# S5 stage of a two-layer diffusion backbone: phase tables summed earlier and loaded, period reordered, inputs ahead of transposes, own residual buffers, modulation products in the GLU stage

## The chip, the cores and the metric

The kernel runs on one core of one Trainium2 chip. The metric is the device time of one execution in microseconds (us). The core has five engines with in-order queues: PE (TensorE, matmuls; PEld is its weight load), DVE (VectorE), ACT (ScalarE), POOL (GpSimd) and SP (SyncE), which here issues every DMA. "L1806" is line 1806 of the kernel before.

## The reference

Two layers over 1024 latent tokens with 256 context tokens in front, 1024 channels, in fp32. Layer 0 mixes tokens with differential attention, layer 1 with a bidirectional S5 state-space scan and a GLU; each mixer is followed by a squared-ReLU MLP (1024 to 4096 to 1024). Cut to what the change touches:

```python
for i in range(2):
    mod_l = silu(c) @ ada_w[i] + ada_b[i]           # six vectors of 1024: sh1 s1 g1 sh2 s2 g2
    h = rmsnorm(x, g0) * (1 + s1) + sh1
    y = attention(h) if i == 0 else s5_mixer(h)
    x = x + g1 * rmsnorm(y, g1n)
    h = rmsnorm(x, g2n) * (1 + s2) + sh2
    x = x + g2 * rmsnorm(square(relu(h @ w1)) @ w2, g3n)

# s5_mixer, for both directions d, 64 groups of 16 channels, 64 complex states per group
h_t = lam_bar * h_{t-1} + B u_t                     # recurrence over time
y   = Re(C h_t) summed over d, + D * u
g   = gelu(y);  o1, o2 = split(g @ w_glu);  return o1 * sigmoid(o2)
```

The kernel cuts time into chunks of 8 tokens (so 160 chunks, context first) and turns the complex recurrence over chunks into a real one: the chunk inputs are rotated by minus a phase (theta times the chunk index), scanned with a real decay, and rotated back. That is why the kernel needs, for each group of four state rows, a table of phases and its sine and cosine.

## The kernel before, in words

The stages run one after the other: attention; the first MLP's up part (`mlp0_up`, matmuls against w1 with hi/lo split operands: L132 to L134 are the three products of such a split, L137 and L138 make the two halves of an operand on ACT and DVE); its down part (`mlp0_down`); the S5 scan (`s5`); the GLU (`glu`); the second MLP up and down. Around the matmuls, `self.bg` holds generators of background work, of which a step is emitted after each piece of main work. The order on the engines is chosen by a scheduler, except inside `with self.manual()`, where the written order is kept; only SP's order is still chosen there.

**Phases.** In `mlp0_down` the background step `s5_phases` (L1199) lets POOL fill two int32 tables by doubling additions (L1209, L1212, L1214): A (128 x 10) and B (128 x 16) for each partition. They go to device memory (`ptd`, 13 KB per partition, 1.7 MB) and come back before `s5`. A phase table of one period n and direction d, 128 x 640, is then made inside `s5` by one POOL addition of broadcast slices, A + B (`phase`, L1777). There are three buffers for phases and their cosines (`phs`).

**The period.** `s5` runs n = 0 to 15 (four groups each), plus a tail for the GELU. For each n and d:
- `trig` (ACT, L1781 to L1784): sine of the half phase, sine, square, and 1 - 2 times it, which is the cosine. `decay` (ACT, L1811) fills the scan's decay.
- `inputs(n, d)` (PE, L1797): 8 matmuls, each two passes in the trace, into two PSUM banks.
- `rotate(n, d)` (DVE, L1806): PSUM inputs times cosine and times sine, into t1 and t2. Then POOL adds them (L1887 for d = 0, L1896 for d = 1).
- `scan` (DVE, L1815), from t1 into t2 with the decay.
- `back` (L1823): t2 times cosine on DVE, t2 times sine on POOL.

`outputs(n)` (PE, L1829 and L1832) multiplies the rotated-back states of both directions with C and adds the direct term. The GELU of period n - 2 follows (ACT L1870, L1883, L1889; DVE L1882, L1904), then four PE transposes (`tr`, L1836) and a split of the result (ACT L1840, DVE `lo` L1841), which is the GLU's operand.

The two directions have separate t1 buffers per parity of n, but d = 0 has one t2 for both parities (FD 12.5), and so has d = 1 (FD 20).

**Modulation of layer 1.** Its segments 2 to 5 (g1, sh2, s2, g2) are eight halves of 1024 x 512 each. Each is loaded in four pieces of 512 KB into one of two sets of buffers and multiplied by 32 small fp32 matmuls (L247, 64 passes in the trace), copied (L251), transposed (L254) and added into `modc` (L256). They stand in the periods n = 8 to 17, after `outputs` and ahead of `tr`.

**From `mlp0_down` to `s5`.** Ten row tiles (two of context, eight latent) are normalised by steps of `m0_tile`: `residual` (L1710) writes y = w * r + x; `second` (ACT L1715 and DVE or POOL L1716) squares y and writes w = y * A; `modulate` (L1719) writes y = w * r + B **into the same y** whose value the residual step stores to `xb` by DMA. So `modulate` waits until that store has landed. Four 32 x 32-block transposes (L1678) put the result into U, which `inputs` reads. The last two tiles, 6 and 7, use W 12 and H 52 for x.

**GLU.** `glu` runs two groups of four row tiles; in each, four column blocks nb with 24 matmuls per tile (L132 to L134) and their operands' splits. The row g1 is spread to all partitions at its start (`rows_out`, `row_bc`).

Of the kernel before, what the change touches and what calls it, by code (L numbers as in the profile page):

```python
# [6 lines left out]
F32 = mybir.dt.float32  # L7
F32R = mybir.dt.float32r
I32 = mybir.dt.int32
# [61 lines left out]
class Prog:  # L71
# [171 lines left out]
    def ada_half_products(self, ws, l, seg, half, acc, t=None):  # L243
# [5 lines left out]
        if t is None:  # L249
            t = self.adat[:, 0:128]  # L250
            nc.scalar.activation(t, acc, AF.Copy)  # L251
        else:
            nc.vector.tensor_copy(t, acc)
# [696 lines left out]
    def s5_prep(self):  # L950
# [67 lines left out]
        self.dma(self.phd, pc)  # L1018
# [180 lines left out]
    def s5_phases(self, o):  # L1199
# [3 lines left out]
        B, P, P16 = (self.fv(x, *d).bitcast(I32) for x, d in ((o, (128, 16)), (o + 8, (128,)), (o + 8.5, (128,))))  # L1203
        self.dma(self.fv(o + 9, 128), self.phd)
        nc.vector.tensor_copy(P, self.fv(o + 9, 128))
# [11 lines left out]
        fill(B, 16, P)  # L1217
        g(P16, B[:, :, 8], B[:, :, 8], ALU.add)
        self.dma(self.ptd[:, 5 * KB : 13 * KB], B.rearrange("p a b -> p (a b)"))
        yield  # L1220
        A = self.fv(o, 128, 10).bitcast(I32)
        fill(A, 10, P16)
        self.dma(self.ptd[:, 0 : 5 * KB], A.rearrange("p a b -> p (a b)"))
        yield
# [8 lines left out]
    def phase_c(self):  # L1233
        nc, I = self.nc, self.I
# [259 lines left out]
    def mlp0_up(self):  # L1494
# [8 lines left out]
                                   [self.rows_out(1, acc)], [self.w2_sums(fu(17.5, 2, 1024))])]  # L1503
        for p in range(self.HEAD // 2, 16):
# [76 lines left out]
    def mlp0_down(self):  # L1581
# [6 lines left out]
        self.bg = [self.s5_phases(40), self.s5_tables(0, self.bank(3), self.bank(2))]  # L1588
# [67 lines left out]
    def m0_buffers(self, i):  # L1656

        f, w = lambda x: self.fv(x, 1024), lambda: self.wv(12, 1024)
        h = lambda: self.hv(52, 1024).bitcast(F32)
        return {0: lambda: (f(40), f(44)), 1: lambda: (f(48), f(52)), 2: lambda: (h(), w()), 3: lambda: (f(40), f(44)),  # L1660
                8: lambda: (f(52), w()), 9: lambda: (h(), f(52)), 4: lambda: (w(), f(0)), 5: lambda: (h(), f(4)),
                6: lambda: (w(), f(8)), 7: lambda: (h(), f(12))}[i]()
# [17 lines left out]
    def m0_tile(self, i, b=None):  # L1680
# [28 lines left out]
        def residual():  # L1709
            v.scalar_tensor_tensor(y, w, r, x, ALU.mult, ALU.add)  # L1710
            if i < 8:
                self.tile_dma(self.xb, i, y, store=True)

        def second():
            act.activation(junk, y, AF.Square, scale=1.0 / 32, accum_out=ms)  # L1715
            (pool if i in (9, 5) else v).tensor_tensor(w, y, A, ALU.mult)  # L1716

        def modulate():
            v.scalar_tensor_tensor(y, w, r, B, ALU.mult, ALU.add)  # L1719
# [15 lines left out]
    def s5(self):  # L1735
# [10 lines left out]
        At, Bt = self.fv(42.5, 128, 10).bitcast(I32), self.fv(47.5, 128, 16).bitcast(I32)  # L1746
# [559 lines left out]
```

## Time and profile before

| | us |
|---|---|
| measured, 3 runs | 2934.82, 2941.13, 2941.93 (median 2941.13) |
| profiled execution, first to last instruction (span) | 2929.2 |
| the median less that span (work around the span) | 11.9 |
| `mlp0_up` | about 1080 to 1455 |
| `mlp0_down`, to its last product | about 1455 to 1870.5 |
| first rotation of `s5` | 1893.91 |
| last rotation pair of n = 15, d = 0 | 2074.93 |
| last transposes of `s5` end | 2101.3 |
| first GLU matmul | 2102.94 |

The page gives the span alone for the profiled execution; its own device time is taken as the span with the same 11.9 us around it, that is 2941.1 us, equal to the median. A row of the windows view gives, for a stretch of the span, the busy time of each engine (with its count of instructions), the granted TensorE clock, the share of time in which the 16 DMA engines were busy, and GB/s. A row of the timeline gives start, length, engine, line, operation, output <- input, shape, and in brackets how long the engine was idle before it and what it waited for. A row of groups gives all instructions of one line and shape with their busy time and mean length in ns. Over the whole span PE is busy 2739.6 us (94%), DVE 2021.3 (69%), ACT 1367.5 (47%) and POOL 1062.1 (36%).

### The profile page before, as it was taken

Reading aid. Unit: us, or ns where it says so; the run is one execution under the profiler, and the core shown is the slowest. Engines: PE = TensorE matmul, PEld = TensorE weight load, DVE = VectorE, ACT = ScalarE, POOL = GpSimd, SP = SyncE. Lnnn points to the kernel's source line nnn. Section 1 sums busy time; section 2 is a strip of 40 time slices with the busy share of each in tenths; the row PEclk is TensorE's granted clock in tenths of the full one; section 3 lists DMA queues with packets and bytes.
Section 4 is the critical chain, followed back from the end, with each engine's and each line's share of the span. In section 5 each row is a group of like instructions: output and inputs, shape, how many; then the busy total and the mean of one; then the engine's idle time right before and its main releaser. Section 6 shows DMA issues by size and latency. Waiting matters only on the chain.

```text
span 2929.2 us, 43646 instructions
## 1 busy us (share of the span) xinstructions
PE 2739.6 (94%) x15200; PEld 2287.5 (78%) x15200; DVE 2021.3 (69%) x2956; ACT 1367.5 (47%) x2555; POOL 1062.1 (36%) x923
## 2 busy tenths in 40 slices
PE   5998999999988999999999999688899899999999
PEld 3687888788777887878877778588788678878887
DVE  5355777777764477676688768699743687758566
ACT  3424555555553663333444435377543643345443
POOL 2213666666553700000020004499410543326324
PEclk8999999999989999999999999899999999999999
DMA  9956455555744448886699988468834254467544
GB/s 250 292 181 205 139 164 169 162 149 162 220 145 152 140 152 303 303 291 243 228 299 293 274 241 258 153 200 264 282 124 136 72 175 159 148 213 256 159 139 141
DMA packets 454122, 588.44 MB, mean 201 GB/s; under 512 B 62742, under 2 KB 299532, under 8 KB 450700
## 3 DMA queue, kind: packets, MB, share of 16 engines
q1 hardware_dynamic: 453900, 585.63, 63.6%
q8 instruction: 120, 1.97, 0.3%
q14 instruction: 102, 0.84, 0.1%
HBM read 398.48 MB, written 182.82 MB: 198 GB/s over the span
## 4 chain that ended last, share of the span: by engine, by line
PE 66%; DMA 12%; DVE 10%; issue 4%; ACT 4%; SPq 2%; POOL 2%; DVEq 0%; ACTq 0%; POOLq 0%
PE PS L132 19%; PE PS L133 18%; PE PS L134 18%; SPq L80 2%; PE PS L520 2%; PE PS L1797 2%; ACT F L543 2%; PE PS L1832 1%; PE PS L566 1%; DVE F L533 1%; DVE R L138 1%; DVE H L138 1%; PE PS L202 1%; DMA U<-in_mlp_w 1%; DMA U<-Aa 1%
## 5 line engine op out<-in xcount | busy, mean ns | idle before, releaser
L132 PE MATMUL PS<-H 128*128 128x512 f32 x1048 | 412.0, 395 | 7.7 <-DVE FD L1604 5.0
L133 PE MATMUL PS<-H 128*128 128x512 f32 x1048 | 410.4, 392 | 0.0
L134 PE MATMUL PS<-H 128*128 128x512 f32 x1048 | 409.8, 392 | 0.0
L132 PE MATMUL PS<-H,R 128*128 128x512 f32 (+1 forms) x836 | 311.2, 378 | 18.5 <-ACT F L579 13.7
L133 PE MATMUL PS<-H,R 128*128 128x512 f32 (+1 forms) x836 | 303.8, 363 | 1.1 <-POOL H L138 1.1
L134 PE MATMUL PS<-H,R 128*128 128x512 f32 (+1 forms) x836 | 303.6, 364 | 0.0
L137 ACT ACTIVATE R<-W 128x512 fp32r<-128x512 f32 (+1 forms) x203 | 142.9, 711 | 208.7 <-PE PS L133 114.9
L132 PEld LDWEIGHTS PS<-H 128*128 128x128 f32 x1048 | 197.9, 189 | 52.4 <-DVE FD L1604 5.3
L134 PEld LDWEIGHTS PS<-H 128*128 128x128 f32 x1048 | 197.7, 189 | 42.5 <-issue 1.0
L133 PEld LDWEIGHTS PS<-H 128*128 128x128 f32 x1048 | 197.9, 189 | 41.2 <-issue 1.2
L132 PE MATMUL PS<-R,H 128*128 128x512 f32 x532 | 214.7, 407 | 7.4 <-ACT H L137 6.0
L543 ACT ACTIVATE F<-F,stat 128x1280 f32<-128x1280 f32 x128 | 174.3, 1362 | 83.8 <-DVE F L533 83.5
L133 PE MATMUL PS<-R,H 128*128 128x512 f32 x532 | 210.8, 397 | 0.0
L134 PE MATMUL PS<-R,H 128*128 128x512 f32 x532 | 208.3, 395 | 0.0
L137 ACT ACTIVATE H<-U 128x640 fp32r<-128x640 f32 x216 | 132.8, 677 | 144.2 <-PE PS L133 110.7
L132 PEld LDWEIGHTS PS<-H,R 128*128 128x128 f32 x836 | 160.7, 193 | 47.6 <-ACT F L579 15.1
L138 DVE TENSOR_TENSOR H<-W,H 128x512 fp32r<-128x512 f32 (+1 forms) x137 | 128.6, 949 | 93.6 <-ACT H L137 93.6
L138 DVE TENSOR_TENSOR R<-W,R 128x512 fp32r<-128x512 f32 (+1 forms) x166 | 150.8, 915 | 60.8 <-ACT R L137 53.5
L533 DVE TENSOR_SCALAR_CACHE_REDUCE F<-PS 128x1280 f32<-128x1280 f32 x128 | 185.1, 1482 | 9.1 <-PE PS L520 8.9
L138 DVE TENSOR_TENSOR H<-U,H 128x640 fp32r<-128x640 f32 x216 | 163.4, 793 | 39.5 <-ACT H L137 39.3
L580 POOL TENSOR_SCALAR R<-F 128x256 fp32r<-128x256 f32 (+1 forms) x128 | 122.8, 959 | 172.1 <-ACT F L579 149.1
L134 PEld LDWEIGHTS PS<-H,R 128*128 128x128 f32 x836 | 160.7, 192 | 25.9 <-issue 0.8
(477 smaller groups left out, 6818.0 us busy)
## 6 DMA issues: line engine op xcount, KB each, us to landing
W<-in_mlp_w SPq DMA_DIRECT2D x184, 256.0 KB, 3.1
U<-Aa SPq DMA_DIRECT2D x108, 320.0 KB, 5.0
Aa<-FU SPq DMA_DIRECT2D x91, 320.0 KB, 4.6
Ad<-F SPq DMA_DIRECT2D x112, 256.0 KB, 3.2
W<-Ad SPq DMA_DIRECT2D x112, 256.0 KB, 2.8
W<-in_ada_w SPq DMA_DIRECT2D x32, 512.0 KB, 6.9
FU<-in_mlp_w SPq DMA_DIRECT2D x32, 512.0 KB, 6.3
Ta<-FU SPq DMA_DIRECT2D x16, 1024.0 KB, 5.6
```

The costliest lines, as they stand in the source:

```text
L80: return self.nc.sync.dma_start(out=out, in_=in_)
L132: mm(out, ah, bh, start=first, stop=False, **kw)
L133: mm(out, ah, bl, start=False, stop=False, **kw)
L134: mm(out, al, bh, start=False, stop=last, **kw)
L137: self.nc.scalar.activation(hi, src, AF.Copy)
L138: (lo_eng or self.nc.vector).tensor_tensor(lo, src, hi.bitcast(F32), ALU.subtract)
L202: self.nc.tensor.matmul(acc[32 * j : 32 * j + 32, 0:256], self.scT[:, 2 * k : 2 * k + 32], w[:, 256 * j : 256 * j + 256], start=k == 0, st ...
L520: mm(self.PS[:, 1280 * c + k0 : 1280 * c + k1], Q[:, c, r, qs], K[c][:, k0:k1], start=r == 0, stop=r == 1)
L533: ts(p[c], self.PS[:, 1280 * c : 1280 * c + 1280], 1.0, None, ALU.mult, ALU.min, accum_out=sm[:, c : c + 1])
L543: nc.scalar.activation(p[c], p[c], AF.Exp, bias=sm[:, c : c + 1], scale=-1.0, accum_out=sn[:, 0:1] if c else s0[:, u + 1 : u + 2])
L580: nc.gpsimd.tensor_scalar(hi, t, 1.0, 0.0, ALU.mult, ALU.add)
L1797: mm(b[:, o : o + 160], X[:, d, i, 64 * j : 64 * j + 128], U[:, 4 * n + i, cols], start=True, stop=True)
```

## The change

Five edits, made together. Line numbers in the rows of instructions are each kernel's own.

1. **Phases.** `s5_phases` moves to the end of `mlp0_up`'s background list. For each direction it fills A and B (half as wide), then makes all sixteen phase tables by POOL additions into a ring of three buffers and stores each (320 KB) to `phd`. In `s5`, `phase` is a DMA load of that table into one of five buffers. `ptd` is gone.
2. **Cosine.** `trig` has three ACT operations in place of four: absolute value, sine, and sine of (pi/2 - |x|). The table for them is set at the start of `phase_c`, ahead of `mlp0_up`.
3. **Order of the period.** The scan and rotation back of direction 1 go to the next period, behind its rotation of direction 0; `inputs(n + 1, 0)` follow `outputs(n - 1)` and stand ahead of `tr`; t2 of d = 0 has a buffer per parity.
4. **Residual buffers.** `residual` writes w and stores w; `second` and `modulate` write y. Tiles 6 and 7 read x from U 48 and U 58. For tiles 4, 6 and 7 w is FD 0, FD 8 and FD 12, which `s5` uses for a phase table and for t2.
5. **Modulation.** The eight halves leave `s5`; in the GLU's first group there is one ahead of each odd tile, on one set of four buffers, and `rows_out` runs after the second and the eighth.

```diff
@@ s5_phases, now in mlp0_up's background
+        for d in range(2):
+            fill(B, 16, P[:, 64 * d : 64 * d + 64])
+            g(P16, B[:, :, 8], B[:, :, 8], ALU.add)
+            fill(A, 10, P16)
+            yield
+            for n in range(16):
+                t, x = out.next(), slice(4 * n, 4 * n + 4)
+                g(t, bcast(A[:, x], 3, 16), bcast(B[:, x], 2, 10), ALU.add)
+                self.dma(self.phd[2 * n + d], t.rearrange("p x a b -> p (x a b)"))
+                if n % 2:
+                    yield
...
+        self.bg.append(self.s5_phases(fu))
...
-        self.bg = [self.s5_phases(40), self.s5_tables(0, self.bank(3), self.bank(2))]
+        self.bg = [self.s5_tables(0, self.bank(3), self.bank(2))]
@@ m0_tile
-            v.scalar_tensor_tensor(y, w, r, x, ALU.mult, ALU.add)
+            v.scalar_tensor_tensor(w, w, r, x, ALU.mult, ALU.add)
             if i < 8:
-                self.tile_dma(self.xb, i, y, store=True)
+                self.tile_dma(self.xb, i, w, store=True)
...
-            v.scalar_tensor_tensor(y, w, r, B, ALU.mult, ALU.add)
+            v.scalar_tensor_tensor(y, y, r, B, ALU.mult, ALU.add)
@@ s5
-            pool.tensor_tensor(P.rearrange("p x (a b) -> p x a b", b=16), bcast(a, 3, 16), bcast(b, 2, 10), ALU.add)
+            self.dma(phs[(2 * n + d) % 5][0].bitcast(I32).rearrange("p x n -> p (x n)"), self.phd[2 * n + d])
...
-            act.activation(Pc, Ps.bitcast(I32), AF.Sin, scale=0.5 * UNPHASE)
+            act.activation(Pc, Ps.bitcast(I32), AF.Abs, scale=UNPHASE)
             act.activation(Ps, Ps.bitcast(I32), AF.Sin, scale=UNPHASE)
-            act.activation(Pc, Pc, AF.Square)
-            act.activation(Pc, Pc, AF.Copy, scale=-2.0, bias=1.0)
+            act.activation(Pc, Pc, AF.Sin, scale=-1.0, bias=quarter)
@@ glu
+                    if g == 0 and t % 2:
+                        self.ada_half_products(hw, 1, *halves[2 * nb + t // 2], self.bank(5)[:, 0:128],
+                                               self.adat[:, 0:128], True)
...
+                    if g == 0 and t % 2:
+                        i = 2 * nb + t // 2
+                        self.ada_half_end(1, *halves[i], self.bank(5)[:, 0:128], self.adat[:, 0:128])
+                        if i < 7:
+                            self.ada_half_load(hw, 1, *halves[i + 1])
```

The first place is DVE in one period of `s5`. Before (names: FD holds phases, t1, t2 and rotated-back states; H or W the weights and split results; U the decay and GELU results):

```order
L1806 TENSOR_TENSOR FD<-PS,FD 128x640 x2
L1841 SCALAR_TENSOR_TENSOR H<-PS,H 128x512
L1882 SCALAR_TENSOR_TENSOR FD<-FD,PS 128x512
L1806 TENSOR_TENSOR FD<-PS,FD 128x640 x2
L1815 SCALAR_TENSOR_TENSOR FD<-U,FD 128x640
L1904 TENSOR_TENSOR U<-FD,PS 128x4x8x16
L1823 TENSOR_TENSOR FD<-FD 128x512
L1815 SCALAR_TENSOR_TENSOR FD<-U,FD 128x640
L1823 TENSOR_TENSOR FD<-FD 128x4x128
```

And the same engine now, where L1811 is the rotation, L1820 the scan, L1828 the rotation back, L1846 `lo`, L1894 and L1913 the GELU:

```order
L1811 TENSOR_TENSOR FD<-PS,FD 128x640 x2
L1820 SCALAR_TENSOR_TENSOR FD<-U,FD 128x640
L1828 TENSOR_TENSOR FD<-FD 128x4x128
L1846 SCALAR_TENSOR_TENSOR H<-PS,H 128x512
L1894 SCALAR_TENSOR_TENSOR FD<-FD,PS 128x512
L1811 TENSOR_TENSOR FD<-PS,FD 128x640 x2
L1820 SCALAR_TENSOR_TENSOR FD<-U,FD 128x640
L1828 TENSOR_TENSOR FD<-FD 128x512
L1913 TENSOR_TENSOR FD<-FD,PS 128x4x8x16
```

The scan and rotation back of direction 1 moved from the end of the period to a place behind the next period's first rotation pair; the nine operations are the same. On POOL the period had six operations, two phase additions, two sums and two rotations back, and now has four:

```order
L1823 TENSOR_TENSOR FD<-FD 128x4x128
L1777 TENSOR_TENSOR FD<-FD 128x640
L1887 TENSOR_TENSOR FD<-FD 128x640
L1896 TENSOR_TENSOR FD<-FD 128x640
L1823 TENSOR_TENSOR FD<-FD 128x512
L1777 TENSOR_TENSOR FD<-FD 128x640
```

```order
L1828 TENSOR_TENSOR FD<-FD 128x4x128
L1850 TENSOR_TENSOR FD<-FD 128x640
L1828 TENSOR_TENSOR FD<-FD 128x512
L1850 TENSOR_TENSOR FD<-FD 128x640
L1828 TENSOR_TENSOR FD<-FD 128x4x128
```

The two L1777 rows are gone, and the two sums (now L1850) stand apart; the last row is the next period's first. The second place is PE in one period of `s5`, before; L1829 and L1832 are `outputs` (of its four pairs of rows the last is shown), L1836 the transposes and L1797 `inputs` of both directions in one run:

```order
L1829 MATMUL PS<-W,U 128x128
L1832 MATMUL PS<-W,FD 128x128 x4
L1836 MATMUL PS<-ident,FD 128x128 x4
L1797 MATMUL PS<-U,W 128x160 x16
L1829 MATMUL PS<-H,U 128x128
```

And now, with `outputs` in L1834 and L1837, `inputs` in L1802 and the transposes in L1841:

```order
L1834 MATMUL PS<-W,U 128x128
L1837 MATMUL PS<-W,FD 128x128 x4
L1802 MATMUL PS<-U,W 128x160 x8
L1841 MATMUL PS<-ident,FD 128x128 x4
L1802 MATMUL PS<-U,W 128x160 x8
L1834 MATMUL PS<-H,U 128x128
```

Half of the inputs, those of direction 0 of the next period, moved ahead of the transposes. The third place is PE at the start of the GLU now; L132 to L134 are the GLU's products with R and H, L247 the modulation's with the buffers `hw` (F) and silu(c) (scT):

```order
L1841 MATMUL PS<-ident,FD 128x128 x8
L132 MATMUL PS<-R_16598,H 128x512 x4
L247 MATMUL PS<-F_16599,scT 32x128 x8
L133 MATMUL PS<-R_16598,H 128x512
L134 MATMUL PS<-R_16598,H 128x512
L132 MATMUL PS<-R_16598,H 128x512
```

Before, no L247 row stood behind the last transposes; now the first eight products of the modulation stand behind four products of the GLU, and the other GLU products behind them.

More of the change, by code (lines that the diff above doesn't have):

```diff
@@ L1854, in s5 @@
                     pool.memset(rs[d][i][:, :, 0:1], 0.0)
-            phase(0, 0)
-            phase(0, 1)
             trig(0, 0)
             decay(0, 0)
+            inputs(0, 0)
             load_x(1)
```

141 lines of the change are left out of this document (65 added, 76 removed).

## Prediction

> **What bounds the kernel now.** I read the windows view first, one row per stretch, to see which engine has no slack in each stage that the change touches.
>
> ```profile
> core 0: us, PE busy (x) PEld busy (x) DVE busy (x) ACT busy (x) POOL busy (x), PEclk, DMA share, GB/s
> ...
> 1360.00:1450.00 90.00, 90.00 (x466) 77.37 (x465) 56.67 (x84) 34.92 (x71) 0.00 (x0) 1.00 0.57 198
> ...
> 1450.00:1475.00 25.00, 25.00 (x126) 19.87 (x125) 21.88 (x34) 10.95 (x19) 0.86 (x2) 1.00 0.96 313
> ...
> 1463.00:1510.00 47.00, 45.23 (x241) 35.19 (x241) 44.67 (x60) 22.84 (x43) 19.65 (x17) 1.00 0.97 301
> ...
> 1930.52:1988.19 57.67, 50.18 (x380) 48.11 (x380) 57.08 (x55) 44.77 (x71) 56.06 (x31) 0.97 0.73 217
> 1988.19:2074.93 86.74, 79.09 (x853) 75.27 (x854) 84.68 (x88) 65.65 (x106) 79.59 (x43) 0.98 0.94 284
> ...
> 2120.00:2270.00 150.00, 150.00 (x664) 124.20 (x662) 56.62 (x69) 59.29 (x106) 16.21 (x21) 1.00 0.39 127
> ```
>
> The first MLP's tail (1360 to 1450) and the GLU (2120 to 2270) are bound by PE without a gap. The S5 stage is not: over five periods (1930.52 to 1988.19, 11.53 us each) PE has 7.5 us free, while DVE is busy 57.08 and POOL 56.06 of 57.67. In the next seven periods 86.74 us pass, 6.0 more than seven times 11.53, with 321 more PE instructions than 7 x 76: five modulation halves of 64 passes.
>
> Then one period in the timeline, to see whether DVE is full with work or with waiting.
>
> ```profile
> 1976.66 1.54 DVE L1806 TENSOR_TENSOR FD<-PS,FD 128x640 f32<-128x640 f32 x2
> 1977.52 1.35 PE L1797 MATMUL PS<-U,W 128*128 128x160 f32 x8 [1.78 <-DVE FD L1806]
> 1978.12 0.68 DVE L1841 SCALAR_TENSOR_TENSOR H<-PS,H 128x512 fp32r<-128x512 f32 x1
> 1978.85 0.49 PE L1829 MATMUL PS<-H,U 128*128 128x128 f32 x2
> 1979.31 1.54 DVE L1806 TENSOR_TENSOR FD<-PS,FD 128x640 f32<-128x640 f32 x2
> 1980.78 1.48 DVE L1815 TENSOR_TENSOR_SCAN FD<-U,FD 128x640 f32<-128x640 f32 x1
> 1980.94 2.68 POOL L1896 TENSOR_TENSOR FD<-FD 128x640 f32<-128x640 f32 x1 [0.20 <-DVE FD L1806]
> 1982.18 0.66 DVE L1904 TENSOR_TENSOR U<-FD,PS 128x512 f32<-128x512 f32 x1
> 1982.76 1.41 DVE L1823 TENSOR_TENSOR FD<-FD 128x512 f32<-128x512 f32 x1
> 1983.42 0.60 PE L1836 MATMUL PS<-ident,U 128*128 128x128 f32 x4
> 1983.57 1.74 POOL L1823 TENSOR_TENSOR FD<-FD 128x512 f32<-128x512 f32 x1
> 1983.86 3.42 PE L1797 MATMUL PS<-U,H 128*128 128x160 f32 x24
> 1984.09 2.56 DVE L1815 TENSOR_TENSOR_SCAN FD<-U,FD 128x640 f32<-128x640 f32 x1
> 1985.38 2.33 POOL L1777 TENSOR_TENSOR FD<-FD 128x640 int32<-128x640 int32 x1
> 1986.68 1.58 DVE L1823 TENSOR_TENSOR FD<-FD 128x512 f32<-128x512 f32 x1
> 1988.19 0.81 DVE L1806 TENSOR_TENSOR FD<-PS,FD 128x640 f32<-128x640 f32 x1
> ```
>
> ```profile
> 2084.95 0.69 DVE L1823 TENSOR_TENSOR FD<-FD 128x512 f32<-128x512 f32 x1
> 2085.08 1.69 POOL L1823 TENSOR_TENSOR FD<-FD 128x512 f32<-128x512 f32 x1 [1.52 <-DVE FD L1815]
> ```
>
> The same operations have two lengths. The first scan, begun before POOL's sum, takes 1.48 us; the second, begun behind POOL's rotation back, 2.56. DVE's rotation back is 1.41 and 1.58 here and 0.69 where POOL started later. Each long one ends only after the POOL operation ahead of it: DVE and POOL exclude each other when both operands of DVE's operation lie in SBUF; those with an operand in PSUM (L1806, L1841, L1904) keep their length. From start to start the eight DVE rows take 1.46, 1.19 (with one more GELU operation in it), 1.47, 1.40, 0.58, 1.33, 2.59 and 1.51, together 11.53. With both scans at 1.40 and both backs at 0.6 it would be 8.7: of the 11.53 us, 2.8 are DVE waiting for POOL.
>
> The Trainium skill ("SBUF — State Buffer", section "SBUF: two separate sides") has this as a rule: DVE and GpSimd share a port pair as an exclusive lock, and of a DVE operation with two SBUF inputs and a GpSimd operation the one that starts first holds it for its whole length. The trace agrees (1.48 against 2.56 us).
>
> **The change, part by part.**
>
> *Phases leave POOL (s5).* Two POOL additions (1.27 to 2.33 us, 2.33 in the row) go from each period. What stays on POOL are two sums and two rotations back, 4 x about 1.5 = 6 us. Excluding work is then 4.0 on DVE (2 x 1.40 + 2 x 0.6) and 6 on POOL, 10 in all, some of which still meets. DVE alone needs 8.7. So PE comes next: outputs 1978.85 to 1983.42 is 4.57, transposes 0.44, inputs 32 passes at 3.42 / 24 = 0.14, 4.4: 9.4 us. PE cannot run without gaps, since the new order has a loop: `outputs(n-1)` 4.57 (less its first six passes, 0.8, which need only direction 0), `inputs(n+1, 0)` 2.2, the second half of their rotation 0.8, the scan of direction 1 1.4, both rotations back 1.85 (2084.95 to 2085.08 + 1.69), then the next outputs: 10.0, and about 0.4 of hand-overs. I take **10.4 us per period**. Bounds: 9.4 (PE alone) and 11.53 (nothing gained). 16 x 1.13 = **-18 us**. ACT's saved operation (0.74 of 9 us busy) and the earlier activation table lie beside DVE; they cost and save nothing in the period. If the DVE cover went, ACT's 8.2 us per period (44.77 / 5 less 0.74) would still be under 9.4.
>
> The phases' cover is DMA: 32 x 320 KB = 10.5 MB go into the stage, 0.65 MB on top of 217 GB/s x 11.53 us = 2.5 MB (in which some modulation loads are counted; they leave). At 10.4 us that is at most 300 GB/s, against 313 in the row 1450:1475, the highest shown. It fits barely, with two periods of notice.
>
> *Modulation leaves s5.* Five halves cost 6.0 us there, and three more stand in the tail after 2074.93.
>
> ```profile
> L247 PE MATMUL PS<-U,scT 128*32 128x128 f32 x512 | 15.6, 274 | 0.0
> ...
> L254 PE MATMUL PS<-ident,adat 128*128 128x128 f32 x8 | 2.6, 328 | 4.4 <-ACT adat L251 4.4
> ```
>
> Groups of the stage: 512 passes are 15.6 us, 1.95 per half, and a transpose 0.33. The last three cost up to 3 x 2.3 = 6.9, and 4.4 us of waits for ACT beside; I take 4, since a part lies beside the GELU's chain. **-10 us** (bounds -6 and -13).
>
> *Modulation enters the GLU.* PE is busy 150.00 of 150.00 there, so all of it is on the path: 15.6 + 2.6 = 18.2. The first half's products stand behind four GLU products, and their load, into buffers that `s5` uses to its end, is issued only then. The nearest DMA row is 6.9 us to landing for 512 KB pieces (below), and the four products cover 4 x 150 / 664 = 0.9, so up to 6 us of waiting; behind it are all other GLU products. Only the first 512 KB are needed at first, so I take 2: **+20 us** (bounds 18 and 30: the upper if each later half, 2 MB in two tiles of 24 products, also comes 1 us late).
>
> ```profile
> W<-in_ada_w SPq DMA_DIRECT2D x32, 512.0 KB, 6.9
> ```
>
> *Phases in the MLP's tail.* POOL is idle there now (0.00 in 1360 to 1450). It gets 32 additions at 1.27 and twice the fills. The fills now stand at 1463 to 1510: 19.65 us of POOL, in which PE had 45.23 of 47, a loss of 1.77. New POOL work is 40.6 + about 24 (twice as many fill operations, half as wide) = 64 us, 3.3 times as much: 5.8, less the 1.8 that goes. **+4 us**. From below: 0, since DVE has 33 us free of 90 and nothing needs a phase before 1880; or -2, if only the relief at 1463 counts. From above: 62 POOL operations that each hold a DVE operation for their whole length of 1.27 are 79 us against 33 free, and with half of the 46 left falling on PE: +23. The stores, 10.5 MB at 313 GB/s, are 34 us of DMA; 43% of 90 us is free there, 39 us, so they fit if they go out in time; `ptd`'s store and reload (3.4 MB, 11 us) go from the stretches at 0.97.
>
> By the lock rule of the same page, POOL's 64 us and DVE's two-input operations could not overlap at all in the tail: this is the rule that speaks against the change. What it would give is the upper bound just named, and it is a rival below.
>
> *Residual buffers and the way into s5.*
>
> ```profile
> 1877.74 1.28 DVE L1710 SCALAR_TENSOR_TENSOR FD<-FD,tl,H 128x1024 f32<-128x1024 f32 x1 [0.36 <-DMA H<-xa]
> ...
> 1880.21 1.01 ACT L1715 ACTIVATE PS<-FD 128x1024 f32<-128x1024 f32 x1
> ...
> 1881.43 1.16 POOL L1700 TENSOR_SCALAR tl<-tl 128x1 f32<-128x1 f32 x1 [3.64 <-DVE U L1678]
> ...
> 1882.66 3.02 SPq L80 DMA_DIRECT2D xb<-FD  x4
> ...
> 1885.92 1.28 DVE L1719 SCALAR_TENSOR_TENSOR FD<-FD,tl,W 128x1024 f32<-128x1024 f32 x1 [3.39 <-DMA xb<-FD]
> ...
> 1889.28 1.28 DVE L1719 SCALAR_TENSOR_TENSOR FD<-FD,tl,W 128x1024 f32<-128x1024 f32 x1 [2.08 <-DMA xb<-FD]
> ...
> 1893.91 0.82 DVE L1806 TENSOR_TENSOR FD<-PS,FD 128x640 f32<-128x640 f32 x1 [0.82 <-PE PS L1797]
> ```
>
> The last two `modulate` wait 3.39 and 2.08 us for their stores, and PE waits for them. Without this wait tile 7's could start when its root is done: POOL's steps from 1881.43 take 1.16 and 0.55, so 1883.2 in place of 1889.28, 6 us; the square (1880.21) follows the residual (ends 1879.02) about a microsecond sooner without the table load and one trig operation, and tiles 6 and 7 have x earlier (0.36): **-8 us**. What is late next: the first rotation's second half writes t2 in FD 12.5, where tile 7's stored value lies. Its store, issued right after the residual ends (1878 by then), with the 7.29 us of the chain row below, lands at 1885.5, just when rotation would come (1885.9). Issued as late as now, at 1882.66, it lands at 1890, and the gain is 3. Bounds -10 and 0.
>
> ```profile
> 1878.51 7.29 DMA xb<-FD
> ```
>
> Sum: -18 - 10 + 20 + 4 - 8 = **-12**. Against the profiled execution's own time, 2929.2 of span and 11.9 around it, equal to the median of 2941.1, this is **2929 us**.
>
> **The rivals.**
>
> *A. POOL blocks DVE in the first MLP (slower).* Place: 1360 to 1510. Price: +23 on the tail in place of +4, and a further 5 where the additions run on into the stretch after 1450, in which DVE has only 3 of 25 us free. It decides from the point at which POOL's operations take the 33 us that DVE has free, about 26 full blocks of 1.27. For it: the 2.56 us scans. Against: PE lost only 1.77 beside 19.65 us of POOL. Time: -18 - 10 + 20 + 28 - 8 = +12, 2953.
>
> *B. Loads become the wait.* The phase loads queue on SP behind loads that wait for PE, or the later modulation halves come late. The period stays at 11.0 (-8 in place of -18) and the GLU costs 24: -8 - 10 + 24 + 4 - 8 = +2, 2943. For it: DMA is at 0.94 in 1988 to 2075. Against: the modulation's 16 MB leave that stretch.
>
> *C. The residual wait is only moved.* The rotation waits for the store in modulate's place: the 8 us shrink to 1: -5, 2936. For it: FD 12.5. Against: a store issued sooner.
>
> *D. More gain.* The period is 9.6 (PE nearly full), -31; the rest as forecast but for the tail at 0: -31 - 10 + 20 - 8 = -29, 2912. Against: the loop above.
>
> **How the numbers follow.** Forecast 0.42, A 0.25, B 0.15, C 0.07, D 0.11. The forecast's own range is 2919 to 2939. Some 0.3% (9 us) is what a measurement can tell from no change: below 2932.3 is faster, above 2950 slower. Faster: 0.35 of the forecast, D's 0.11, and 0.04 of B and C: 0.50. Slower: most of A, 0.21, and 0.04 of B: 0.25. Same: 0.25. The range runs from D's side, 2908, to A's with something of the GLU's bound, 2957.
>
> **What would show it.** Right: rotations 10.2 to 10.6 us apart, scans near 1.5, PE over 90% in the stage; first rotation at about 8 us less than now, measured from the last product of the MLP; a GLU longer by 20 with PE gaps of 2 at most; the MLP's two parts together longer by 4. Wrong: rotations that wait for a phase DMA or its ACT operations (B); PE gaps before 1510 that end with DVE splits (A); a first rotation pair split by a wait for `xb` (C).

## The result and the profile after

The change made no difference that the measurement can tell: median 2940.46 us over 20 runs (2934.13 to 2955.55) against 2939.86 over 20 runs of the kernel before (2927.52 to 2948.81), a ratio of 1.0009 with the 95% interval 0.9997 to 1.0022. The forecast was 2929 us (2908 to 2957): its likeliest case, faster by 12 us, did not come true.

One correction first. The profiled execution of the changed kernel took 2943.8 us with a span of 2942.0, so 1.8 us lie around the span, not the 11.9 us that the prediction took. The profile of before was therefore an execution of about 2931 us, nine below its median. Both kernels were profiled a second time (among the experiments below), and the table gives both executions. A stage runs from one matmul to the same matmul of the other kernel (the n-th of the 10428 matmuls at L132 to L134, which are the same work in both); the S5 stage runs from the first rotation to the end of the last transposes. The row "GLU" ends in the GLU's second group of tiles, behind all eight halves.

| stage, us | before | before again | changed | changed again |
|---|---|---|---|---|
| attention | 916.9 | 919.7 | 921.0 | 916.6 |
| output projection, head of the first MLP | 123.1 | 123.8 | 128.2 | 126.1 |
| first MLP, up part without its tail | 278.0 | 278.9 | 276.9 | 280.4 |
| its tail (1318 to 1434 in before) | 116.3 | 117.3 | 126.7 | 127.7 |
| rest of the up part, down part to the last product | 436.3 | 437.0 | 437.9 | 439.6 |
| last product to first rotation | 23.2 | 23.9 | 17.4 | 16.7 |
| S5 | 207.4 | 206.5 | 185.7 | 181.3 |
| GLU | 139.9 | 139.9 | 161.1 | 160.7 |
| the rest (end of GLU, second MLP) | 688.0 | 691.6 | 687.1 | 685.6 |
| span | 2929.2 | 2938.7 | 2942.0 | 2934.7 |

Stages with the same instructions differ by up to 4.4 us between executions of one kernel. Beyond that, S5 gained 21 to 26 us, the way into it 6 to 7; the GLU lost 21 and the MLP's tail 9 to 11. The output projection lost 2 to 5. The down part looks 1 to 3 longer, which is not beyond its spread: over all kernels here it takes 436.1 to 440.2, and two without phase additions in the MLP (below) have 437.9 and 437.8.

The windows of the changed kernel for the stretches that the prediction quoted, and five periods of S5 (10.55 us each):

```profile
1360.00:1450.00 90.00, 82.52 (x421) 69.85 (x419) 68.46 (x75) 28.44 (x62) 69.47 (x66) 0.98 0.70 255
1986.78:2039.53 52.75, 47.60 (x383) 46.40 (x382) 45.91 (x56) 38.22 (x61) 31.95 (x22) 1.00 0.86 261
2120.00:2270.00 150.00, 150.00 (x1023) 122.74 (x1012) 54.56 (x77) 55.93 (x100) 16.81 (x18) 1.00 0.62 206
```

In the first row PE has 7.5 us idle where it had none, and POOL, which was at 0.00, is busy 69.47 of 90. In the second, DVE fell from 99% to 87% and POOL from 97% to 61%, and PE rose from 87% to 90%: DVE is no longer full. In the third PE is still full, with 1023 instructions in place of 664.

One period in the timeline of the changed kernel (L1811 is the rotation, L1820 the scan, L1828 the rotation back, L1846 `lo`, L1834 the first products of `outputs`):

```profile
1982.72 0.82 DVE L1811 TENSOR_TENSOR FD<-PS,FD 128x640 f32<-128x640 f32 x1 [0.19 <-PE PS L1802]
1983.46 1.48 DVE L1820 TENSOR_TENSOR_SCAN FD<-U,FD 128x640 f32<-128x640 f32 x1
1984.98 0.69 DVE L1828 TENSOR_TENSOR FD<-FD 128x512 f32<-128x512 f32 x1
1985.17 1.64 POOL L1828 TENSOR_TENSOR FD<-FD 128x512 f32<-128x512 f32 x1 [2.49 <-DVE FD L1820]
1985.59 0.68 DVE L1846 SCALAR_TENSOR_TENSOR H<-PS,H 128x512 fp32r<-128x512 f32 x1
1986.33 0.49 PE L1834 MATMUL PS<-H,U 128*128 128x128 f32 x2 [1.03 <-DVE H L1846]
1988.36 1.49 DVE L1820 TENSOR_TENSOR_SCAN FD<-U,FD 128x640 f32<-128x640 f32 x1
1989.88 0.69 DVE L1828 TENSOR_TENSOR FD<-FD 128x512 f32<-128x512 f32 x1
1992.25 0.82 DVE L1811 TENSOR_TENSOR FD<-PS,FD 128x640 f32<-128x640 f32 x1 [1.08 <-PE PS L1802]
```

Both scans are 1.48 and 1.49 us now (1.48 and 2.56 before) and both rotations back 0.69 (1.41 and 1.58). POOL waits for DVE, where DVE waited for POOL. PE's one gap in a period is 1.03 us, and it ends with `lo`. In n = 2 and 3, before `lo` begins, the period is 10.19 us.

And the place where the time went, the MLP's tail (POOL's phase additions, and beside them DVE):

```profile
1384.04 5.23 POOL L1229 TENSOR_TENSOR FU<-FU 128x640 int32<-128x640 int32 x3
...
1384.55 1.90 DVE L1446 TENSOR_TENSOR FU<-FU 128x640 f32<-128x640 f32 x1
1386.37 1.76 DVE L1403 TENSOR_TENSOR W<-W 128x512 f32<-128x512 f32 x1
1388.05 1.77 DVE L138 TENSOR_TENSOR R<-W,R 128x512 fp32r<-128x512 f32 x1
...
1394.80 0.68 DVE L1538 TENSOR_TENSOR FU<-PS,FU 128x512 f32<-128x512 f32 x1
...
1396.71 1.76 DVE L1539 SCALAR_TENSOR_TENSOR FU<-FU 128x512 f32<-128x512 f32 x1
```

An operation of DVE that reads SBUF twice takes up to 1.76 us where it took 0.69 (L1529 before, now L1539); L1538, which reads PSUM, keeps its 0.68. The groups from 1375 to 1450, first of before, then of the changed kernel, give the means:

```profile
L1529 DVE SCALAR_TENSOR_TENSOR FU<-FU 128x512 f32<-128x512 f32 x9 | 6.2, 688 | 0.1
```

```profile
L1539 DVE SCALAR_TENSOR_TENSOR FU<-FU 128x512 f32<-128x512 f32 x6 | 9.1, 1524 | 0.1
```

The additions are stretched as well:

```profile
L1229 POOL TENSOR_TENSOR FU<-FU x32: 1273/1722/1857, 1381.1 to 1447.3; 128x640 int32<-128x640 int32 x32
```

Their shortest is 1.27 us, their median 1.72: the two engines take turns, and each pays for the other. PE's idle time from 1375 to 1460 ends with operations that empty a PSUM bank, on ACT and on DVE; before, PE had no such wait in the tail:

```profile
PE PS L132 <- ACT FU L1525: 4.6, 3, 1.8
PE PS L132 <- DVE FU L1538: 2.8, 2, 1.9
```

### The profile page after: what moved, and what is told of

Its sections match the earlier page's. It is cut to its first block, busy times and chain, and to the rows that moved or that the text cites. A ratio compares the mean times of both kernels' runs of the same rounds, so it can differ in the third digit from the quotient of the medians.

```text
span 2942.0 us, 43782 instructions
## 1 busy us (share of the span) xinstructions
PE 2751.6 (94%) x15201; PEld 2294.0 (78%) x15201; DVE 1990.9 (68%) x2957; ACT 1345.1 (46%) x2522; POOL 1036.6 (35%) x941
## 5 line engine op out<-in xcount | busy, mean ns | idle before, releaser
L132 PE MATMUL PS<-H 128*128 128x512 f32 x1048 | 411.2, 394 | 4.3 <-DVE FD L1614 2.7
L134 PE MATMUL PS<-H 128*128 128x512 f32 x1048 | 409.0, 391 | 1.9 <-DVE H L138 1.9
L132 PE MATMUL PS<-H,R 128*128 128x512 f32 (+1 forms) x836 | 313.1, 380 | 19.4 <-ACT F L582 14.0
L134 PE MATMUL PS<-H,R 128*128 128x512 f32 (+1 forms) x836 | 306.0, 367 | 0.0
L132 PEld LDWEIGHTS PS<-H 128*128 128x128 f32 x1048 | 197.3, 188 | 49.4 <-issue 6.2
L134 PEld LDWEIGHTS PS<-H 128*128 128x128 f32 x1048 | 197.4, 188 | 44.0 <-DVE H L138 2.8
L132 PE MATMUL PS<-R,H 128*128 128x512 f32 x532 | 216.2, 410 | 7.0 <-ACT H L137 5.4
L134 PE MATMUL PS<-R,H 128*128 128x512 f32 x532 | 208.4, 395 | 0.0
L138 DVE TENSOR_TENSOR R<-W,R 128x512 fp32r<-128x512 f32 (+1 forms) x166 | 155.4, 943 | 69.2 <-ACT R L137 61.6
L132 PEld LDWEIGHTS PS<-H,R 128*128 128x128 f32 x836 | 162.1, 194 | 48.3 <-ACT F L582 15.4
L138 DVE TENSOR_TENSOR H<-W,H 128x512 fp32r<-128x512 f32 (+1 forms) x137 | 132.9, 980 | 92.9 <-ACT H L137 92.7
L138 DVE TENSOR_TENSOR H<-U,H 128x640 fp32r<-128x640 f32 x216 | 160.0, 777 | 41.1 <-ACT H L137 39.8
L134 PEld LDWEIGHTS PS<-H,R 128*128 128x128 f32 x836 | 162.5, 194 | 26.1 <-POOL R L138 0.9
```

What stands on the lines that cost most here:

```text
L132: mm(out, ah, bh, start=first, stop=False, **kw)
L134: mm(out, al, bh, start=False, stop=last, **kw)
L138: (lo_eng or self.nc.vector).tensor_tensor(lo, src, hi.bitcast(F32), ALU.subtract)
```

## Experiments

**Theory 1:** the phase sums gained what was forecast in S5 and lost it in the MLP's tail, by POOL and DVE excluding each other there; modulation only changed its place, from a stage that PE did not fill to one that it does. **Rivals:** the tail's loss comes from the 10.5 MB of stores, or from another order of its matmuls; the new order of the period, not POOL's relief, made S5 shorter; edit 4's wait was on the path, or was only moved.

**Modulation back in S5.** Edit 5 is taken back: the halves stand in the periods n = 8 to 17 again, and the GLU has none. The place of the products:

```diff
...
+                for i, (a, b) in enumerate(mods):
+                    if n == b:
+                        self.ada_half_products(halves[i % 2 if i > 2 else 0], 1, 2 + i // 2, i % 2, self.PS[:, 1856:1984], t, True)
+                        self.ada_half_end(1, 2 + i // 2, i % 2, self.PS[:, 1856:1984], t)
                 if 3 <= n < 19:
                     tr((n - 3) // 2, 1 - n % 2, bank)
...
```

> The changed kernel with edit 5 taken back: the eight modulation halves stand in the S5 periods n = 8 to 17 again, ahead of the transposes, and the GLU has none. Theory 1 (the GLU has no PE gap, the S5 stage has about 1.0 us per period): the GLU gets shorter by about 21 us, the figure by which it grew, and the S5 stage grows by less, 10 to 16 us, since a half of 2.3 us finds 1.0 us of idle PE in its period; in all 5 to 11 us less than the changed kernel. Rival (the new S5 stage is as full of PE work as the GLU): the stage grows by 8 x 2.3 = 18 us or more and nothing is gained.

Measured: GLU 140.8 (20.3 less), S5 205.1 (19.4 more than 185.7, and 23.8 more than the 181.3 of the execution in which the first two periods were as short as here), 2945.57 us, ratio to before 1.0020 (1.0005 to 1.0036). The rival came true: in the new S5 stage the halves cost as much as in the GLU, or more. The row of that stage:

```profile
1990.00:2080.00 90.00, 77.57 (x806) 73.95 (x808) 61.92 (x81) 53.72 (x86) 44.67 (x28) 0.96 0.96 316
```

DMA is busy 96% at 316 GB/s, while PE is at 86% and DVE at 69%. Yet of the waits of PE, DVE, ACT and POOL in this stretch none ends with a DMA. The period with the first half shows what is late (L1804 are the inputs, L1813 the rotation):

```profile
1996.38 2.34 PE L1804 MATMUL PS<-U,W 128*128 128x160 f32 x16
1998.65 1.95 PE L247 MATMUL PS<-U,scT 128*32 128x128 f32 x64
2000.67 0.28 ACT L250 ACTIVATE adat<-PS 128x128 f32<-128x128 f32 x1 [4.17 <-PE PS L247]
2001.00 0.33 PE L257 MATMUL PS<-ident,adat 128*128 128x128 f32 x1 [0.40 <-ACT adat L250]
2001.37 0.17 DVE L259 TENSOR_TENSOR modc<-PS,modc 128x8 f32<-128x8 f32 x1 [4.71 <-PE PS L257]
2001.65 1.55 DVE L1813 TENSOR_TENSOR FD<-PS,FD 128x640 f32<-128x640 f32 x2
```

The inputs of the next rotation are done at 1998.7, but DVE's queue has the additions into `modc` ahead of it. DVE sits idle for 4.71 us, until products, copy and transpose of the half are through, and the rotation starts at 2001.65. This period takes 14.5 us; the next, without a half, takes 11.9 at a granted clock of 0.86, where the one before had 1.00. So by this trace it is the place of the halves in the new order that is dear, and not a wait for transfers.

**Residual written to y again.**

```diff
-            v.scalar_tensor_tensor(w, w, r, x, ALU.mult, ALU.add)
+            v.scalar_tensor_tensor(y, w, r, x, ALU.mult, ALU.add)
             if i < 8:
-                self.tile_dma(self.xb, i, w, store=True)
+                self.tile_dma(self.xb, i, y, store=True)
...
-            v.scalar_tensor_tensor(y, y, r, B, ALU.mult, ALU.add)
+            v.scalar_tensor_tensor(y, w, r, B, ALU.mult, ALU.add)
```

The buffers from which tiles 6 and 7 read x stay as in the changed kernel.

> The changed kernel with the residual written to y, stored from y, and modulation writing y again (edit 4 taken back but for the x buffers of tiles 6 and 7). Theory 1 (modulate's wait for its store was on the path): from the MLP's last product to the first rotation it takes 23 us as before, against 17.4 in the changed kernel, and DVE waits 3 and 2 us for xb again. Rival (the first rotation is held by the phase and weight loads in SP's queue): 17 to 19 us as in the changed kernel.

Measured: 17.5 us to the first rotation (17.4 and 16.7 in the changed kernel), 2938.67 us, ratio 0.9996 (0.9985 to 1.0007). Theory 1 fails here: writing w gains nothing that shows. Waits in the changed kernel, 1893 to 1909:

```profile
POOL tl L1710 <- ACT PS L1725: 8.6, 2, 7.1
ACT FD L1787 <- DMA xb<-FD: 4.1, 1, 4.1
```

Old residual, the same stretch of its own, and from 1880 the wait of its `modulate` (L1729) for the store:

```profile
ACT PS L1725 <- DVE FD L1720: 5.2, 3, 2.6
ACT FD L1787 <- DMA FD<-phd: 4.4, 1, 4.4
...
DVE FD L1729 <- DMA xb<-FD: 1.3, 1, 1.3
```

In the changed kernel DVE's `modulate` does not wait for a store at all, but ACT's first operation on a phase (L1787) does, 4.1 us: its table is loaded into FD 0, where tile 4's stored value lies, and the squares of tiles 6 and 7 (L1725) are queued on ACT behind it, on which POOL and then `modulate` wait 7.1 us. With the old residual `modulate` waits for its store only 1.3 us in all, where it waited 6.2 in the kernel before, and ACT's first operation on a phase is held as long as in the changed kernel, 4.4 us. So most of the wait for the stores had gone without the new buffers.

**The kernel before with edits 1 and 2 alone** (phases made in the MLP and loaded, shorter cosine; old order, residual and modulation):

```diff
...
-            pool.tensor_tensor(P.rearrange("p x (a b) -> p x a b", b=16), bcast(a, 3, 16), bcast(b, 2, 10), ALU.add)
+            self.dma(phs[(2 * n + d) % 5][0].bitcast(I32).rearrange("p x n -> p (x n)"), self.phd[2 * n + d])
...
```

> The kernel before with edits 1 and 2 alone: phases summed in the first MLP and loaded, cosine in three ACT operations; its order of the period, its residual buffers and its modulation in S5 are kept. Theory 1 (POOL's two additions were what DVE waited for): undisturbed periods of 10.0 to 10.6 us against 11.53; the reorder adds little. Rival (the order of PE, inputs behind the transposes, sets the period once DVE is free): 11 us or more. The first MLP's tail and down part are longer by about 12 us in both, as in the changed kernel, if the phase sums cause that.

Measured: undisturbed periods of 10.04 us (n = 2, 3) and 10.63 (n = 4 to 7), where the changed kernel has 10.19 and 10.55. So POOL's relief (with the shorter cosine, which was not tried apart) gives the period, and the new order of edit 3 gives nothing beyond it. But S5 as a whole took 207.7 us, no less than before. DMA is at 1.03 and 312 GB/s from 1990 to 2080, periods take up to 15.8, and from the first rotation of n = 15 to the end of the last transposes it takes 36.2 us, where the kernel before took 26.4. The chain that ended last there goes through the modulation's loads:

```profile
2060.03 12.64 DMA U<-in_ada_w
...
2072.73 10.51 DMA U<-in_ada_w
```

Here the loads are the wait, as in rival B of the prediction. Since the kernel with modulation back in S5 and the new order has no such wait, whether edit 3 or edit 5 keeps it away is open. The MLP's tail was 128.4, the way to the first rotation 20.5. 2942.78 us, ratio 1.0016 (1.0002 to 1.0031).

**The activation table loaded later.**

```diff
     def phase_c(self):
-        self.act_set("silu_and_others")
...
     def mlp0_up(self):
+        self.act_set("silu_and_others")
```

> The changed kernel with the activation table loaded at the start of the first MLP's up part instead of the start of the attention's output projection. Theory 1 (the 1.28 us load there stands on the path, since ACT splits the weights that PE waits for): 1 to 2 us less up to the first MLP, and no other stage changes; too little for the times, read from the trace. Rival (the 4.5 us by which that stage was longer come from the weights' loads): the stage keeps its length.

Measured: 127.2 us for the output projection and head, against 128.2 and 126.1: nothing to be seen in one profile; 2936.72 us, ratio 0.9991 (0.9977 to 1.0005). Over all kernels here, the four with the late table have 122.9 to 127.2 (mean 124.9), the seven with the early one 124.8 to 128.2 (mean 126.5), the kernel before 123.1 and 123.8. A cost of the order of the load itself (1.28 us in the trace) fits, but is not settled.

**No additions.** The 32 POOL additions are left out and the stores kept, of buffers set to zero, so S5 gets no phases:

```diff
...
-                g(t, bcast(A[:, x], 3, 16), bcast(B[:, x], 2, 10), ALU.add)
                 self.dma(self.phd[2 * n + d], t.rearrange("p x a b -> p (x a b)"))
```

> The changed kernel without the 32 POOL additions that sum the phases in the first MLP: the table fills and all 32 stores stay, of buffers that hold zeros (so the S5 output is another one). Theory 1 (POOL's additions and DVE's two-input operations exclude each other, and PE waits for the DVE work that is late): the stretch of the first MLP's tail, 116.3 us before and 126.7 in the changed kernel, falls to 118 or less. Rival 1 (the 10.5 MB of stores and SP's waits for them delay the weights): it stays at 124 or more. Rival 2 (another order of the MLP's matmuls, by the scheduler): it stays about 127 here and without the stores.

**No stores.** All additions, but one store for each direction, and S5 loads that one table for every n:

```diff
-                self.dma(self.phd[2 * n + d], t.rearrange("p x a b -> p (x a b)"))
+                if n == 0:
+                    self.dma(self.phd[2 * n + d], t.rearrange("p x a b -> p (x a b)"))
...
```

> The changed kernel with all 32 POOL additions but only the first store of each direction; S5 loads that one table for every n (so its output is another one). Theory 1 (POOL against DVE): the first MLP's tail stays at 124 us or more, or grows, since the additions no longer wait for their buffers and come closer together. Rival 1 (stores): it falls to 118 or less, and the down part gets shorter too.

Measured: the tail took 115.6 us without additions and 127.4 without stores (116.3 before, 126.7 changed). The windows from 1355 to 1460, first without additions, then without stores:

```profile
1355.00:1460.00 105.00, 105.00 (x537) 89.31 (x536) 71.39 (x103) 37.33 (x75) 20.58 (x35) 1.00 0.78 271
```

```profile
1355.00:1460.00 105.00, 95.26 (x493) 80.18 (x492) 83.47 (x92) 33.12 (x72) 73.24 (x66) 1.00 0.50 175
```

With all the stores and 271 GB/s PE is busy 105.00 of 105; with hardly any store and 175 GB/s, but POOL's additions, it loses 9.7 us, and DVE is busy 83.47 us for 92 operations where it did 103 in 71.39. That settles the tail: it is POOL against DVE, neither the transfers nor another order. Each ran once, in 2926.36 and 2941.68 us.

**Other buffers for the first phases.** The kernel with the late table, and the first two phase tables and the first t1 and t2 moved away from FD 0 to 16:

```diff
-        phs = [(self.fv(x, 4, 160), self.fv(x + 2.5, 4, 160)) for x in (0, 42.5, 7.5, 47.5, 24.5)]
+        phs = [(self.fv(x, 4, 160), self.fv(x + 2.5, 4, 160)) for x in (42.5, 47.5, 0, 7.5, 24.5)]
...
-              for p in (((5, 12.5), (29.5, 53)), ((15, 20), (17.5, 20)))]
+              for p in (((29.5, 53), (5, 12.5)), ((15, 20), (17.5, 20)))]
...
```

> The changed kernel with the activation table loaded at the start of the first MLP, and with the first two phase tables in FD 42.5 and 47.5 and the first t1, t2 of direction 0 in FD 29.5 and 53, away from the stored values of tiles 4 to 7. Theory 2 (edit 4 moved the wait for the xb stores from modulate to the first phase load, on which ACT's first operation waits 4.1 us with the squares of tiles 6 and 7 queued behind): from the MLP's last product to the first rotation 12 to 14 us against 17.4. Rival (DVE's chain of residual, square, root, modulation and transposes sets it): 16 to 17.4.

Measured: 16.5 us to the first rotation. The wait of L1787 for `xb` is gone from the list of waits, and still the stretch is only 0.2 to 0.9 shorter. That fits the rival, the chain from residual over square, root and modulation to the transposes; DVE itself waits 4.6 us in it for POOL's root. That this chain sets the length is read from what is left, and was not tried. 2938.16 us, ratio 0.9990 (0.9976 to 1.0003).

**Two halves in S5's tail.** The last kernel with the two halves of segment g1 ahead of the last transposes, six left in the GLU:

```diff
...
+                if n == 17:
+                    for i in range(2):
+                        t, acc = self.adat[:, 128 * i : 128 * i + 128], self.PS[:, 1856 - 512 * i : 1984 - 512 * i]
+                        self.ada_half_products(early[i], 1, 2, i, acc, t, True)
+                        self.ada_half_end(1, 2, i, acc, t)
...
```

> The kernel of f3_first_phases, and two of the eight modulation halves (g1) moved from the GLU to the end of the S5 stage, between the last outputs and the last transposes, where PE is idle for 4.0 us of GELU; the other six stay in the GLU. Theory 1 (a half costs 2.6 us where PE is full and nothing where it waits): the GLU is 5 us shorter than in the changed kernel, 156, and the S5 stage's end as long as before or 1 us longer. Rival (the copies and transposes of the halves delay the GELU chain as in the kernel before): the S5 stage grows by 4 or more and nothing is gained.

Measured: GLU 155.1 (161.1 and 160.7 in the changed kernel, 162.1 in the last), S5 183.9 (185.7 and 181.3, 184.9). The end of S5, from the first rotation of n = 15, takes 29.8 us, 2.0 more than in the last kernel: the halves stand on PE for 6.3 us (2080.31 to 2086.65), where it waited 4.1 in the last kernel. So Theory 1 holds but for those 2 us: 6 to 7 us less in the GLU, 2 more in S5. 2936.02 us, ratio to before 0.9983 (0.9969 to 0.9996).

**Phases summed in the attention stage.** The last kernel, with one POOL operation of the fills or one addition per step of the attention's loop, in 12.25 KB of buffers of their own:

```diff
+                if n >= 2:
+                    next(phases, None)
                 for part in range(3):
                     if part < parts:
...
     def mlp0_up(self):
...
-        self.bg.append(self.s5_phases(fu))
```

> The kernel of f4_two_halves_in_tail with the phase tables summed in the attention stage instead of the first MLP's tail: one POOL operation of the fills or one of the 32 additions per step of the attention's loop, where POOL waits about 2 us per step for ACT and DVE's longest operations read PSUM. Theory 1 (only the meeting with DVE's two-input operations made the sums dear): the MLP's tail falls back from 126.7 to 116 us, the attention grows by 0 to 6, in all 5 to 11 us less than f4_two_halves_in_tail, 0.993 to 0.997 of the kernel before. Rival (POOL's queue is on the attention's path, so each operation of about 1.3 us is paid there too): the attention grows by 20 us or more and the kernel is slower than f4_two_halves_in_tail.

Measured: the tail 117.2 us, the attention 917.3 (916.3 to 921.7 in all the others but one, which has 914.7), 2924.34 us, **ratio to before 0.9949 (0.9932 to 0.9966)**. The additions cost nothing there. Their group from 100 to 800 us:

```profile
L1238 POOL TENSOR_TENSOR Z<-Z 128x640 int32<-128x640 int32 x31 | 39.6, 1276 | 0.0
```

They take 1276 ns on average, as the shortest in the MLP's tail: nothing of DVE holds them there. And the tail's row is as before:

```profile
1355.00:1460.00 105.00, 103.52 (x530) 87.90 (x529) 70.98 (x109) 40.16 (x83) 0.00 (x0) 1.00 0.60 203
```

This version beats the kernel before. It was not run beside the changed kernel, but that one's interval (0.9997 to 1.0022) lies apart from this one.

**Both kernels again**, unchanged, for the spread between executions; their stages are in the first table.

> The kernel before, unchanged, in another execution, to see how far its stages differ between executions. Theory (the profile of before was a fast execution: its span is 2929 where the median of 35 runs is 2939): the attention, up to the output projection, takes 917 to 922 us and the output projection and MLP head 123 to 127, and the stages from the MLP's tail to the GLU repeat within 1 or 2 us. Rival (the stages that the change touches vary as much as the attention): they differ by 4 us or more.

> The changed kernel, unchanged, in another execution, for the same purpose: the MLP's tail 126 to 128 us, from the MLP's last product to the first rotation 17 to 18, S5 182 to 186 (the first two periods depend on the granted clock), GLU 160 to 162.

Measured: 2940.51 and 2936.5 us. The MLP's tail, the way into S5 and the GLU repeat within 1 us, and so does S5 of the kernel before. S5 of the changed kernel (185.7 and 181.3) does not: its first two periods take 21.6 and 17.9 us.

## Why the prediction was right or wrong

The sum was -12 us, and +2.6 was measured. The time lies within the range because the range took in the rivals; the likeliest case itself missed, above all by the phases in the MLP's tail (+10 in place of +4), then by S5, which gained 3 to 6 less than forecast. The start of the sum, 11.9 us around the span where 1.8 were measured, did no harm: 2941.1 is close to the median of 2939.86 from 20 runs, which is luck.

**What bounds, right.** POOL's two additions were what DVE waited for. The period fell to 10.55 us from n = 4 on, with 10.4 forecast; 16 x (11.53 - 10.55) is 16 us of the 18. The loop was not quite the one described: PE's gap ends with `lo`, which stands between the rotation back and the outputs and is not in the prediction's loop, and the kernel with edits 1 and 2 alone has the same period without the new order.

**Modulation out of S5, right in the periods and wrong in the tail.** S5 as a whole gained 21.7 us (25.2 by the second pair of profiles) of the 28. The 6.0 us in the periods came: from the first rotation of n = 2 to that of n = 15 it took 155.95 us before and takes 136.44 now, which is 13.5 by shorter periods in these 13 steps and 6.0 by the halves. The 4 us of the tail did not come: from the first rotation of n = 15 to the end of the last transposes it took 26.4 and 26.3 us before and takes 27.7 and 27.0 now. The new order leaves one more scan and rotation back to this stretch; what that costs was not tried apart. The prediction priced the halves by the old stage. In the new one they would have cost 19.4 to 23.8, by the chain that holds up the rotation, which the prediction did not have.

**Modulation into the GLU, right.** +21.2 and +20.8 against +20. The wait for the first load, taken as 2 us, was 0.3. What came in its place is a dearer half: 17.1 us of L247 in place of 15.6. PE's idle time beside the products is this one wait of 0.3; the rest of the 21 is PE at work.

```profile
L247 PE MATMUL PS<-F,scT 128*32 128x128 f32 x512 | 17.1, 279 | 0.3 <-DMA F<-in_ada_w 0.3
```

**Phases in the MLP's tail, the term that failed.** +4 was forecast, +10.4 measured in the tail; the 1 to 3 us behind it are not shown to come from the phases. The mechanism was that of rival A, the bound of +23 held, and the forecast took the value of the nearest row. That row (1463 to 1510) was near in kind and far in density: POOL was busy 19.65 of 47 us there, with a gap of 12.1, and DVE could go on in the gaps. In the tail POOL is busy 69.5 of some 77 us, so that most DVE operations with two SBUF inputs meet an addition: L1539 takes 1.52 us on average in place of 0.69, the splits of L138 some 1.1 in place of 0.7. Scaling the loss by POOL's busy time was the mistake. DVE's busy time grew by 12 us, well within the 33 of 90 that were free, and still PE lost 7.5 there: free time of DVE in the sum does not help if an operation that PE needs is late. That the density of POOL's work is what matters is argued from these two rows; no run varied it in the tail. The sign named for A, gaps that end with DVE's splits, was not the one seen: PE's gaps end with ACT and DVE operations that empty PSUM banks.

**Residual buffers, right in size and wrong in cause.** -8 was forecast, -5.8 and -7.2 measured, and the kernel that writes y again has it too. The wait of `modulate` for the stores and the length of the stretch fall together: 6.2 us and 23.2 before, 4.7 and 20.5 with edits 1 and 2, 1.3 and 17.5 with the old residual, none and 17.4 in the changed kernel. That bears out that the wait was on the path, but it was not writing w that took most of it away. Rival C is seen at another spot than FD 12.5, in ACT's wait for the first phase; with that gone too, 16.5 us are left. About 3 of the 6 us come with edits 1 and 2, which also take two table loads of 1.28 us each out of this stretch; the other 3 lie between that kernel and the one with the old residual, which differ in the x buffers of tiles 6 and 7, in the order and in the modulation. Which of these it is was not tried.

**Not in the sum:** the output projection and head, 2 to 5 us longer. The table load may be part of it; the cause is open.

The terms as measured in the two pairs of profiles are -21.7 and -25.2 (S5), +21.2 and +20.8 (GLU), +10.4 twice (tail), +1.6 and +2.6 (down part), -5.8 and -7.2 (way into S5), +5.1 and +2.3 (projection): +11 and +4 us. In the times it is 0.09% (2.6 us, interval -0.9 to 6.5). The second MLP was 1 to 6 us shorter in these profiles, and its spread over all kernels here is 685.6 to 693.0.

## What to carry to other kernels

Work that is moved off a full engine should be priced where it arrives: look there for what it excludes, and whether it comes in one dense run. The same 32 additions cost some 16 us in S5, 11 in the MLP's tail and nothing that shows in the attention, where they come one per step and DVE's longest operations read PSUM; which of the two makes them free was not tried. Small work for PE belongs where PE waits for a chain of other engines: two halves of modulation cost 2 us behind the last outputs and 6 to 7 in the GLU. And its whole chain counts, not its products alone: ahead of the rotation, five halves made the periods of the new order 21 us longer.

## What the runs showed of the hardware

POOL and DVE, each with a run of SBUF operations, take turns one by one in the rows from 1384 on: additions went from 1.27 to 1.72 us in the median, DVE's from 0.69 to as much as 1.76. DVE operations with an operand in PSUM stayed at 0.68 beside them. The Trainium skill ("SBUF — State Buffer", section "SBUF: two separate sides") states this lock, and the trace agrees; that both sides are stretched when both are dense is what the runs add.

The first two periods of S5 took 21.6 and 17.9 us in two executions of the changed kernel, with the same instructions in the same order. The windows of these periods, first of the one, then of the other:

```profile
1908.00:1915.60 7.60, 7.60 (x47) 7.60 (x47) 5.33 (x7) 1.88 (x3) 2.13 (x2) 0.82 0.21 72
1915.60:1929.70 14.10, 10.78 (x62) 10.18 (x61) 7.48 (x10) 3.37 (x6) 9.20 (x6) 0.76 0.42 126
```

```profile
1907.04:1913.69 6.65, 6.65 (x47) 6.65 (x47) 5.30 (x6) 1.04 (x2) 2.10 (x2) 0.93 0.21 73
1913.69:1924.89 11.20, 7.87 (x61) 7.28 (x60) 7.48 (x9) 3.36 (x6) 7.94 (x6) 1.00 0.48 151
```

The granted clock is 0.82 and 0.76 in one, 0.93 and 1.00 in the other, and PE's busy time differs by as much as the periods do, 3.9 us. In the slower one the clock falls a second time: it is 0.50 from 1904 to 1910, after 15 us of idle PE, 1.00 from 1911 to 1921, and 0.50 again from 1922 to 1927, behind 2 us (1919 to 1921) in which PE was busy 0.31. In the other PE was busy 0.18 of such 2 us (1917 to 1919), and the clock stayed at 1.00. So some four microseconds at the start of S5 come and go between executions, and no difference between kernels should be read from them.
